# One number in a planner's price list: what a float32r matmul is said to cost

## The chip, the cores and the metric

The kernel runs on one core of a Trainium2 chip. The metric is the device time of one execution in microseconds (us), as the median of several runs; smaller is better. The engines are PE (TensorE: matmul), with its weight load PEld, DVE (VectorE), ACT (ScalarE), POOL (GpSimd) and SP (SyncE), which here issues the DMAs.

## The reference, cut to what matters

Two transformer blocks of two layers each, one after the other, on 256 tokens of width 1024, all in float32:

```
for i in range(2):                       # first block
    x = x + 0.5*g1 * swiglu(mod(rms(x)), wg, wu, wd)      # F = 2816
    x = x + g2 * (diff_attention(h) if i == 0 else spatial_gating(h))
    x = x + 0.5*g3 * swiglu(mod(rms(x)), wg, wu, wd)
    x = rms_norm(x, ln_out[i])
for i in range(2):                       # second block
    x = x + g1 * (hgrn2_mixer(h) if i == 0 else nsa_mixer(h))
    x = x + g2 * conv_ffn(mod(rms(x)), w_up, conv, w_down)
return rmsnorm(x, final_norm)
```

The shifts, scales and gates (`mod`, `g1` ...) come from `silu(c) @ ada_w`, whose weights are read once like all others.

## The kernel before, in words

The work falls into ten stages: feed-forward (0), differential attention (1), feed-forward (2, 3), spatial gating (4), feed-forward (5), hgrn2 (6), convolutional feed-forward (7), nsa (8), convolutional feed-forward (9). Every projection is computed with float32r operands (a float32 split into a rounded high part and a rest): hi·hi, hi·lo and lo·hi, three products where one would do. ACT copies a loaded weight tile `raw` to `whi`, DVE subtracts to get `wlo`; there are 4 buffers for `raw` and 6 each for `whi` and `wlo`. Activations are split in the same way: `h` to `hhi`, `hlo`, and `a32` or `oT` to `ahi`, `alo`.

Two widths of product occur. Up-projections that keep features on the partitions (`pg`, `pv`, `pa`, `pq`, `pf`, `px`, `pqk`) move 256 columns. Down-projections (`pd`) move 512 columns, as do the kernel's first `pgv`; the products that follow later norms half by half (`pgv`, `pig`, `px`) move 256. Between two stages stands a chain that no PE work of the next stage can pass: the last `pd`, residual on DVE (`gy`, `x`), sum of squares on ACT (`xs`), a power on POOL (`ss`), scaling (`xs`), transposes on PE (`xT`), modulation on ACT (`h`), the split on DVE (`hhi`, `hlo`), then the first product. The 256 tokens are taken in two halves, called first and second half here: `pd` products of the second half are kept back (by the table `SKEW`) so that they lie beside the chain of the first.

None of this is issued in the order in which it is written. Class `Plan` records every operation (`add`), gives it a price in ns (`price`, L289 to L320), and `order` (L322) plays the five engines forward: each engine takes the ready operation that was written first, is busy for its price, and its followers become ready after its end plus a delay from the table `LATE` (L196). Slots for buffers and PSUM tiles, the ACT tables, a DMA rate and a clock model for PE that doubles a price are played too. `emit` (L507) then issues each engine's instructions in the order that came out, which is why every row of the trace has L514 as its line. The hardware runs each engine's queue in that fixed order, with semaphores for what depends on other engines. So a price changes no instruction, only which one stands before which.

The line that is changed is the price of a PE product whose moving operand is float32r (L300 and L301). The other prices of PE stay: a transpose 109 ns, and a float32 product by its rows and columns.

Of the kernel before, what the change touches and what calls it, by code (L numbers as in the profile page):

```python
# [208 lines left out]
class Plan:  # L209
# [79 lines left out]
    def price(self, eng, method, args, kw, reads, writes):  # L289

        n = max(int(np.prod(v.shape[1:])) for v in (writes[-1:] if eng == "tensor" else reads + writes) or reads)
        if eng == "sync":
            v = (writes + reads)[0]
            size = int(np.prod(v.shape)) * 4
            return 450.0, size / 360.0
        if eng == "tensor":
            if method == "transpose":
                return 109.0, 60.0
            n = int(np.prod(args[2].shape[1:]))
            if args[2].tl.dtype == F32R:  # L300
                return n / 2.4 + 2.2, 60.0  # L301
            m = writes[0].shape[0]
            t = 4 * max(n, m) / 2.4
            return (t + 4.5 if m > 64 else t / 2 + 28.0 if m > 32 else t / 4 + 20.0), 60.0
        ps = any(v.tl.psum for v in reads + writes)
        if eng == "scalar":
            aps = sum(isinstance(kw.get(x), Vw) for x in ("scale", "bias", "accum_out"))
            return (51.0 if ps else 94.0) + n * 0.833 + 93.0 * aps, 40.0
        if eng == "gpsimd":
            if kw.get("op") == OP.pow:  # L310
                return 290.0 + 165.0 * n, 60.0
            return 200.0 + 0.7 * n, 60.0
        aps = 0
        if method in ("tensor_scalar", "scalar_tensor_tensor"):
            aps = sum(isinstance(v, Vw) for v in args[2:4 if method == "tensor_scalar" else 3])
        if method in ("tensor_copy", "tensor_scalar", "memset") and not ps:
            return 67.0 + 0.52 * n + 60.0 * aps, 20.0
        if method == "reciprocal":
            return 65.0 + 6.2 * n, 20.0
        return 70.0 + 1.04 * n + 60.0 * aps, 20.0  # L320
# [1626 lines left out]
```

## Time and profile before

| | before |
|---|---|
| median of 3 runs | 1718.03 us (1716.29 to 1719.7) |
| profiled execution | 1716.82 us |
| its span, first to last instruction | 1715.1 us |
| PE busy | 1677.9 us, 98% |
| DVE, ACT, POOL busy | 1309.9, 946.5, 65.3 us |
| mean granted clock of PE | 0.993 |

The profiled execution took 1.7 us more than its span, and 1.2 us less than the median of the runs. A busy engine in this table is one with an instruction in flight; PE's instructions overlap one another, so that the step from one product to the next, not the length of one, is what it costs.

### The profile page before, as it was taken

Reading aid. Unit: us, or ns where it says so; the run is one execution under the profiler, and the core shown is the slowest. Engines: PE = TensorE matmul, PEld = TensorE weight load, DVE = VectorE, ACT = ScalarE, POOL = GpSimd, SP = SyncE. Lnnn points to the kernel's source line nnn. Section 1 sums busy time; section 2 is a strip of 40 time slices with the busy share of each in tenths; the row PEclk is TensorE's granted clock in tenths of the full one; section 3 lists DMA queues with packets and bytes.
Section 4 is the critical chain, followed back from the end, with each engine's and each line's share of the span. In section 5 each row is a group of like instructions: output and inputs, shape, how many; then the busy total and the mean of one; then the engine's idle time right before and its main releaser. Section 6 shows DMA issues by size and latency. Waiting matters only on the chain.

```text
span 1715.1 us, 30950 instructions
## 1 busy us (share of the span) xinstructions
PE 1677.9 (98%) x12662; PEld 1510.6 (88%) x12662; DVE 1309.9 (76%) x1951; ACT 946.5 (55%) x1581; POOL 65.3 (4%) x60
## 2 busy tenths in 40 slices
PE   8999999999999999999999999999999999999998
PEld 6899789889988999789999879989998886689986
DVE  5877688876777888677777787889898557888754
ACT  4544366564445544364544368876554566766542
POOL 0000012100001000000000000000000000000000
PEclk9999999999999999999999999999999999999999
DMA  9988875667886998667689875347898566256662
GB/s 322 346 304 297 291 237 198 211 218 242 304 310 219 330 318 300 240 225 240 215 278 297 304 251 180 127 160 247 272 305 304 176 200 240 79 164 230 220 211 74
DMA packets 258191, 415.25 MB, mean 242 GB/s; under 512 B 12938, under 2 KB 204277, under 8 KB 257025
## 3 DMA queue, kind: packets, MB, share of 16 engines
q1 hardware_dynamic: 258049, 413.27, 71.4%
q8 instruction: 99, 1.62, 0.4%
q14 instruction: 43, 0.35, 0.1%
HBM read 412.14 MB, written 1.10 MB: 241 GB/s over the span
## 4 chain that ended last, share of the span: by engine, by line
PE 87%; DMA 4%; DVE 4%; ACT 3%; issue 1%; SPq 1%; POOL 1%; DVEq 0%; POOLq 0%; ACTq 0%
PE pd L514 22%; PE pv L514 21%; PE pg L514 12%; PE pa L514 7%; PE pgv L514 3%; PE pig L514 3%; PE pq L514 3%; PE pqk L514 2%; PE pf L514 1%; DVE wlo L514 1%; PE px L514 1%; ACT h L514 1%; DMA raw<-in_ffn_wu 1%; ACT whi L514 1%; PE no L514 1%
## 5 line engine op out<-in xcount | busy, mean ns | idle before, releaser
L514 ACT ACTIVATE whi<-raw 128x1024 fp32r<-128x1024 f32 x508 | 531.0, 1056 | 545.2 <-PE pd L514 144.2
L514 DVE TENSOR_TENSOR wlo<-raw,whi 128x1024 fp32r<-128x1024 f32 x508 | 612.0, 1220 | 221.4 <-ACT whi L514 219.1
L514 DVE SCALAR_TENSOR_TENSOR acc<-raw,csil,acc 128x1024 f32<-128x1024 f32 x192 | 245.9, 1281 | 18.1 <-DMA raw<-in_ada_w 15.6
L514 PE MATMUL pv<-hhi,wlo 128*128 128x256 f32 x896 | 252.5, 282 | 0.0
L514 PE MATMUL pv<-hhi,whi 128*128 128x256 f32 x896 | 252.2, 282 | 0.0
L514 PE MATMUL pv<-hlo,whi 128*128 128x256 f32 x896 | 252.1, 281 | 0.0
L514 PE MATMUL pd<-whi,ahi 128*128 128x512 f32 x604 | 238.9, 397 | 1.1 <-ACT ahi L514 0.5
L514 PE MATMUL pd<-wlo,ahi 128*128 128x512 f32 x604 | 238.0, 394 | 0.8 <-DVE wlo L514 0.8
L514 PE MATMUL pd<-whi,alo 128*128 128x512 f32 x604 | 237.3, 394 | 0.0
L514 PE MATMUL pg<-hhi,wlo 128*128 128x256 f32 x608 | 171.8, 283 | 0.7 <-DVE wlo L514 0.7
L514 PE MATMUL pg<-hhi,whi 128*128 128x256 f32 x608 | 172.1, 283 | 0.0
L514 PEld LDWEIGHTS pv<-hhi,whi 128*128 128x128 f32 x896 | 170.6, 190 | 0.8 <-issue 0.8
L514 PE MATMUL pg<-hlo,whi 128*128 128x256 f32 x608 | 171.4, 282 | 0.0
L514 PEld LDWEIGHTS pv<-hhi,wlo 128*128 128x128 f32 x896 | 170.6, 190 | 0.0
L514 PEld LDWEIGHTS pv<-hlo,whi 128*128 128x128 f32 x896 | 170.5, 190 | 0.0
L514 PEld LDWEIGHTS pd<-whi,ahi 128*128 128x128 f32 x604 | 113.4, 188 | 31.9 <-issue 4.5
L514 PEld LDWEIGHTS pd<-wlo,ahi 128*128 128x128 f32 x604 | 113.4, 188 | 26.6 <-DVE wlo L514 1.9
L514 PEld LDWEIGHTS pd<-whi,alo 128*128 128x128 f32 x604 | 113.5, 188 | 25.4
L514 PEld LDWEIGHTS pg<-hhi,whi 128*128 128x128 f32 x608 | 115.8, 190 | 3.0 <-issue 2.1
L514 PEld LDWEIGHTS pg<-hhi,wlo 128*128 128x128 f32 x608 | 115.8, 190 | 0.9 <-DVE wlo L514 0.9
L514 PEld LDWEIGHTS pg<-hlo,whi 128*128 128x128 f32 x608 | 115.7, 190 | 0.0
L514 PE MATMUL pa<-hhi,whi 128*128 128x256 f32 x352 | 99.3, 282 | 0.0
(361 smaller groups left out, 3136.8 us busy)
## 6 DMA issues: line engine op xcount, KB each, us to landing
raw<-in_ada_w SPq DMA_DIRECT2D x118, 1024.0 KB
raw<-in_ffn_wd SPq DMA_DIRECT2D x44, 1024.0 KB
raw<-in_ffn_w_up SPq DMA_DIRECT2D x44, 1024.0 KB
raw<-in_ffn_wg SPq DMA_DIRECT2D x41, 1024.0 KB
raw<-in_ffn_wu SPq DMA_DIRECT2D x41, 1024.0 KB
raw<-in_ffn_w_down SPq DMA_DIRECT2D x22, 1024.0 KB
raw<-in_hg_w_in SPq DMA_DIRECT2D x16, 1024.0 KB
raw<-in_attn_w_qkv SPq DMA_DIRECT2D x12, 1024.0 KB
```

The costliest lines, as they stand in the source:

```text
L514: f(*[real(v) for v in args], **{k: real(v) for k, v in kw.items()})
```

## The change

The price of a float32r product of n columns was n/2.4 + 2.2 ns, and is n/2.4 + 10 + n/78 ns: 108.9 becomes 119.9 ns at n = 256, and 215.5 becomes 229.9 ns at n = 512.

```diff
             if args[2].tl.dtype == F32R:
-                return n / 2.4 + 2.2, 60.0
+                return n / 2.4 + 10.0 + n / 78.0, 60.0
             m = writes[0].shape[0]
```

Each engine issues the same number of instructions of each kind before and after. What differs is their order, in many places on PE, ACT and DVE, in few on SP.

**At the end of attention (stage 1 to 2), PE.** `oT` transposes the last heads' output, `modt` and `modc` belong to the next stage's modulation, `pd` is attention's output projection. Before:

```order
L514 MATMUL pd<-wlo,ahi 128x512
L514 MATMUL o<-v,atT 128x128 x4
L514 MATMUL modt<-ident,sums 128x128 x4
L514 MATMUL pd<-whi,alo 128x512
L514 MATMUL pd<-whi,ahi 128x512
```

Then 13 more rows of `pd`, one product each, up to `oT`, and 25 after it before the transposes `xT` of the next stage. With the change:

```order
L514 MATMUL modc<-acc,ones 32x512 x4
L514 MATMUL pd<-whi,ahi 128x512
L514 MATMUL pd<-wlo,ahi 128x512
L514 MATMUL pd<-whi,alo 128x512
L514 MATMUL pd<-whi,ahi 128x512
L514 MATMUL pd<-wlo,ahi 128x512
L514 MATMUL oT<-ident,on 128x128 x4
L514 MATMUL modt<-ident,sums 128x128 x4
L514 MATMUL pd<-whi,alo 128x512
```

Between `o` and `oT` stand 12 `pd` and `modc` now, where 15 `pd` and `modt` stood, and 43 `pd` follow `oT` before `xT`, where 25 did.

**The same place on DVE**, where `x_96` is the first half of the tokens and `x_103` the second. Before:

```order
L514 TENSOR_TENSOR gy<-pd,gb 128x512
L514 TENSOR_TENSOR x_96<-x_96,gy 128x512
L514 TENSOR_TENSOR gy<-pd,gb 128x512
L514 TENSOR_TENSOR x_96<-x_96,gy 128x512
L514 TENSOR_TENSOR gy<-pd,gb 128x512
L514 TENSOR_TENSOR x_103<-x_103,gy 128x512
L514 TENSOR_SCALAR ss<-ss 128x1
L514 TENSOR_TENSOR gy<-pd,gb 128x512
L514 TENSOR_SCALAR xs<-x_96,ss 128x512
```

With the change:

```order
L514 TENSOR_TENSOR gy<-pd,gb 128x512
L514 TENSOR_TENSOR x_96<-x_96,gy 128x512
L514 TENSOR_TENSOR gy<-pd,gb 128x512
L514 TENSOR_TENSOR x_96<-x_96,gy 128x512
L514 TENSOR_SCALAR ss<-ss 128x1
L514 TENSOR_TENSOR gy<-pd,gb 128x512
L514 TENSOR_SCALAR xs<-x_96,ss 128x512
L514 TENSOR_TENSOR x_103<-x_103,gy 128x512
```

A `gy` and an `x` of the second half stand behind the `ss` of the first.

**At the start of hgrn2 (stage 5 to 6), DVE.** `xrow` is the row scaling of the norm at the end of the first block, `h_10700` and `h_10703` the modulated first half. Before:

```order
L514 TENSOR_TENSOR xrow<-x_103,raw 128x512
L514 TENSOR_TENSOR wlo<-raw,whi 128x1024
L514 TENSOR_TENSOR gy<-pd,gb 128x512
L514 CAST hhi<-h_10700 128x2x128
L514 TENSOR_TENSOR x_103<-x_103,gy 128x512
L514 CAST hhi<-h_10700 128x2x128
L514 TENSOR_TENSOR hlo<-h_10700,hhi 128x4x128
L514 CAST hhi<-h_10710 128x2x128 x2
L514 TENSOR_TENSOR hlo<-h_10710,hhi 128x4x128
L514 TENSOR_TENSOR xrow<-x_103,raw 128x512
L514 TENSOR_SCALAR ss_10681<-ss_10681 128x1
L514 TENSOR_TENSOR wlo<-raw,whi 128x1024
```

With the change:

```order
L514 TENSOR_TENSOR xrow<-x_103,raw 128x512
L514 TENSOR_TENSOR gy<-pd,gb 128x512
L514 TENSOR_TENSOR x_103<-x_103,gy 128x512
L514 TENSOR_TENSOR xrow<-x_103,raw 128x512
L514 CAST hhi<-h_10703 128x2x128 x2
L514 TENSOR_TENSOR hlo<-h_10703,hhi 128x4x128
L514 CAST hhi<-h_10714 128x2x128 x2
L514 TENSOR_TENSOR hlo<-h_10714,hhi 128x4x128
L514 TENSOR_TENSOR wlo<-raw,whi 128x1024 x2
```

(The change has five more rows, `ss`, `x_103` and `xs`, ahead of that last one.) The second half's `x` and `xrow` stand ahead of the first half's split now, and both `wlo` behind it. On PE, 25 `pig`, 8 `xT` and 71 `pig` stand where 47 `pig`, 4 `xT`, 1 `pig`, 4 `xT` and 48 `pig` stood (a single `pf` product among the last).

**In nsa (stage 8), PE.** `ph` is the hidden layer of the compression, `npT` transposes of scores, `pq` a query projection, `pkc` the first product that reads `ht`, the Silu of `ph`. Before:

```order
L514 MATMUL ph<-raw,cw_15273 64x75
L514 MATMUL npT<-ident,lg 128x128 x5
L514 MATMUL pq<-hhi,whi 128x256
L514 MATMUL pq<-hlo,whi 128x256
L514 MATMUL pq<-hhi,wlo 128x256
L514 MATMUL pkc<-ht,cw_14615 64x60
L514 MATMUL pvc<-cw_14615,ht 32x64 x4
```

With the change:

```order
L514 MATMUL pq<-hlo,whi 128x256
L514 MATMUL pq<-hhi,wlo 128x256
L514 MATMUL pq<-hhi,whi 128x256
L514 MATMUL pq<-hlo,whi 128x256
L514 MATMUL pq<-hhi,wlo 128x256
L514 MATMUL pkc<-ht,cw_14617 64x60
L514 MATMUL pvc<-cw_14617,ht 32x64 x4
```

These are the last 5 of 16 `pq` that stand between `npT` and `pkc` now; 13 of them moved there from ahead of `ph`.

## Rows read from the trace of the kernel before

**Rows 1.** The page, busy time, share of the span and instructions of each engine.

```profile
span 1715.1 us, 30950 instructions
PE 1677.9 (98%) x12662; PEld 1510.6 (88%) x12662; DVE 1309.9 (76%) x1951; ACT 946.5 (55%) x1581; POOL 65.3 (4%) x60
```

**Rows 2.** The chain in order of time: start us, us, what; stage 2.

```profile
417.24 5.55 PE pv L514 x48
422.79 5.76 PE pg L514 x48
...
489.01 36.71 PE pd L514 x159
```

**Rows 3.** Waits of PE, whole span: us in total, times, longest.

```profile
PE xT L514 <- DVE xs L514: 4.7, 4, 2.6
...
PE pkc L514 <- ACT ht L514: 1.6, 1, 1.6
...
PE pv L514 <- DVE hhi L514: 0.4, 1, 0.4
```

**Rows 4.** Windows: us, busy us of PE, PEld, DVE, ACT, POOL; PE's clock; DMA.

```profile
348.16:354.99 6.83, 5.73 (x27) 5.73 (x28) 5.04 (x12) 5.61 (x17) 0.56 (x1) 0.50 0.04 6
1440.43:1447.25 6.82, 6.82 (x28) 3.43 (x27) 5.02 (x21) 5.29 (x14) 0.00 (x0) 0.50 0.89 328
```

**Rows 5.** The chain in order of time, stage 1 to 2.

```profile
341.33 0.70 DVE gy L514
...
344.71 0.69 DVE x L514
...
346.25 1.95 ACT xs L514 x5
```

**Rows 6.** Waits of PE from 318 to 356 us.

```profile
PE pd L514 <- ACT ahi L514: 0.5, 1, 0.5
```

**Rows 7.** The chain in attention, first pair of heads.

```profile
249.08 3.56 PE pqk L514 x29
...
256.46 0.11 PE pT L514
```

**Rows 8.** Timeline of DVE, same place: start us, us, engine line op.

```profile
249.10 1.22 DVE L514 TENSOR_TENSOR wlo<-raw,whi 128x1024 fp32r<-128x1024 f32 x1
...
254.60 0.60 DVE L514 SCALAR_TENSOR_TENSOR at<-lg,smx,at 128x128 f32<-128x128 f32 x2
```

**Rows 9.** The chain in order of time, stage 4 to 5.

```profile
824.77 0.73 ACT xs L514
...
825.55 1.09 PE xT L514 x8
```

**Rows 10.** Waits of the DMA queue SP from 880 to 990 us.

```profile
SPq L514 <- ACT grow L514: 2.8, 1, 2.8
```

**Rows 11.** Timeline, stage 5 to 6, [idle before and its releaser].

```profile
1018.63 0.29 DVE L514 CAST hhi<-h 128x256 fp32r<-128x256 f32 x1 [0.23 <-ACT h L514]
...
1022.39 1.22 DVE L514 TENSOR_TENSOR wlo<-raw,whi 128x1024 fp32r<-128x1024 f32 x1
...
1023.66 0.38 PE L514 MATMUL pig<-wlo,hhi 128*128 128x256 f32 x1 [0.50 <-DVE wlo L514]
```

**Rows 12.** The chain in hgrn2, first pair of heads.

```profile
1057.54 1.72 PE pig L514 x13
1059.26 1.34 PE o L514 x12
```

**Rows 13.** Timeline of DVE, same place.

```profile
1057.96 0.92 DVE L514 COPY st<-sc 32x128 f32<-32x128 f32 x4
```

**Rows 14.** Waits of PE from 1150 to 1172 us, stage 6 to 7.

```profile
PE xT L514 <- DVE xs L514: 1.3, 1, 1.3
```

**Rows 15.** The chain in order of time, nsa.

```profile
1436.70 1.28 ACT L514
...
1437.99 0.32 ACT ht L514
```

## The prediction

> **What bounds the kernel now.** First the busy shares: PE has something in flight in 1677.9 of 1715.1 us, and no other engine comes near [rows 1]. So 37 us are all that PE is idle, and most of the rest is products that the change doesn't touch. The waits of PE, taken together next, are small and many: 23 lines, from 4.7 us for `xT` waiting on `xs` down to 0.4 us, which add up to 29 us [rows 3]. The reader is to see that no single wait is worth 0.3% of the time. Third, the clock: in a few stretches the granted clock is 0.50, the 1.2 GHz level; two of them are 6.8 us long, one after the long wait at the end of attention, one in nsa after the wait of `pkc` [rows 4]. With PE busy for 5.73 and 6.82 us in them, half of that, 2.9 and 3.4 us, is what the lower level cost. So what an order can move at all is some 29 us of waits and a handful of us of clock; it can also make new waits, with no such bound, wherever a product that covered a chain is taken away.
>
> **Is the new price right?** 48 products of 256 columns take 5.55 to 5.76 us, which is 116 to 120 ns each, and 159 of 512 columns 36.71 us, or 231 ns [rows 2]. The new price says 119.9 and 229.9, the old said 108.9 and 215.5: the planner believed PE to be 7 to 10% faster than it is. The change does what it says. A rule speaks against it: the Trainium skill, "TensorE: Matmul & The Clock Gate", section "Back-to-back issue gap", gives N/2.4 + 2.5 ns for an isolated product, almost the old price, and for streams of weight load and product about 131 ns at N = 512, far below both. By that page's figure the 159 products would take an estimated 21 us and the change would go the wrong way; this trace has 36.71 us for them, so here the measurement decides, and the price is now right.
>
> A right price for PE doesn't make a right plan. The other prices and delays are as they were, and PE's queue runs in the planned order. With products too cheap, the planner put about 10% more of them between a product that starts a chain on ACT, DVE and POOL and the one that waits for its end, and on the chip that was spare time wherever a chain is longer than planned. The new price takes that spare time away; it also moves work at places where the old plan had a hole. So the sum goes by places. I compared the order on PE, DVE, ACT and SP at each border between stages and inside attention, hgrn2 and nsa. Feed-forward interiors are alike apart from which product follows which, and are put at nothing: there 48 products follow 48 with no wait in the chain.
>
> **The places** (minus is time lost; in brackets both ends).
>
> Start and stage 0 to 1. Three reads of modulation stand one or so 512-column product earlier, 3 x 0.23 = 0.7 us if each waits; `xT` of the second half comes after 34 instead of 37 products, 3 x 0.12 = 0.4. Together -1.1 [0 to -2.2, twice that].
>
> Attention, first pair of heads. From the end of `pl` (249.08) to the end of the `at` that `pT` transposes (255.20) passed 6.1 us, and 57 `pqk` covered them, so that `pT` at 256.46 had 1.3 us to spare [rows 7, 8]. Now 24 `pqk` and two `plam` cover it, 24 x 0.12 + 0.2 = 3.1 us. The chain gets shorter too: the `wlo` of 1.22 us in its middle [rows 8] stands elsewhere, and ACT's table load ahead of it, for which I take another 0.5. That leaves 4.4, and -1.3. Two later pairs have 10 and 5 products fewer: -0.4. Together -1.7 [0 to -3.1, where the chain shortens so little that all 33 products but the 1.3 us are missed].
>
> End of attention. 43 `pd` follow `oT` where 25 did. Before, from the first `gy` (341.33) to the end of its `xs` the chain ran to some 346.6, and DVE did a `gy` and an `x` of the second half (0.6 + 0.69 us) ahead of `ss` in it [rows 5]; `xT` waited 2.6 us of the 4.7 in [rows 3] there. Now those 1.3 us stand behind, which leaves 4.0 us of chain, and some 24 `pd`, 24 x 0.23 = 5.5 us, cover it: +2.6. The wait of `pd` for `ahi`, 0.5 us [rows 6], has `modt` in it: +0.5. The clock fell there after that wait; I count half of its 2.9 us, +1.5. Against that a `wlo` stands between the first two `hhi`, -1.2. Together +3.4 [0 to +6.0, all of wait and clock].
>
> Stage 4 to 5. `xT` of the second half started right when `xs` was there (825.50 against 825.55) [rows 9], so no cover was spare. It comes after 27 instead of 35 products now: 8 x 0.12, -1.0 [0 to -1.0].
>
> Stage 5. SP stood 2.8 us at a store that waited for `grow` [rows 10], with weight loads queued behind it; that store is issued after loads now. Transfers set the end there only in part, so half: +1.4 [0 to +2.8].
>
> Stage 5 to 6. The first `hhi` came at 1018.63; now `x` and `xrow` of the second half, 0.68 us each, stand ahead of it [rows 11], and DVE gets there about 1.1 us later; PE waits for it already, so all of this shows. The `wlo` of 1022.39, on which `pig` waited 0.5 us [rows 11], moves behind the second half's `ss` and `xs`: about 1.3 us later. What comes back is 0.4, since 23 `pig` of the first half are still there to cover the second half's split. Together -2.0 [0 to -4.9, with a half-clock stretch like the first of rows 4, 2.9 us, brought on by the holes].
>
> Heads of hgrn2. In the first pair `st` was complete at 1058.88 and `o` started at 1059.26 [rows 12, 13]: under 0.4 us to spare behind 78 products. 67 are left for the first three pairs, 11 x 0.12 = 1.3 us less. With up to 1.0 to spare elsewhere I take 0.8 for each: -2.4 [0 to -3.9].
>
> Stage 6 to 7. `xT` waits 1.3 us for `xs` [rows 14]; `ss` comes one `gy`, `x` pair earlier: half, +0.7 [0 to +2.0 with some clock].
>
> nsa. `pkc` waits for `ht`, which comes behind ACT's step of 1.28 us at 1436.70 [rows 15]: 1.6 us [rows 3]. 13 more `pq`, 13 x 0.12 = 1.6 us, lie there now: +1.6. Of the 3.4 us of clock after it I count 0.4, since the small products that follow are the same. Together +2.0 [-1.0, since `ph` comes 1.6 us earlier and may wait for its input; to +5.0 with all the clock].
>
> **The sum**: -1.1 - 1.7 + 3.4 - 1.0 + 1.4 - 2.0 - 2.4 + 0.7 + 2.0 = -0.7 us. Against the profiled execution's own 1716.82 (span 1715.1 and 1.7 around it) this is 1717.5. That execution was 1.2 below the median of the runs; on the median, 1718.0 + 0.7 = **1718.7 us**. The lower ends add up to -16, the upper to +16; as the places fail independently, their half-widths (1.1, 1.5, 3, 0.5, 1.4, 2.5, 2, 1, 3) combine to some 6 us, which 8 times in 10 is about 8, and the scatter of a median, 1.7, and the places not read come on top.
>
> **The rivals.** 0.2%, 3.4 us, is about what a measurement of this kernel can tell from no change.
>
> *No change that can be told*, my forecast: PE's products are the same, gains and losses are of one size. Its own range is 1714.6 to 1721.5. Chance 0.38.
>
> *Faster: the two half-clock stretches go with the holes ahead of them.* For it: both follow a wait that the new order covers, by 5.5 us against 4.0, and by 1.6 against 1.6. Against it: in the first, PE is busy for only 5.73 of 6.83 us [rows 4], so later waits lie in it that stay; in nsa the small products stay. It takes the full 2.9 + 3.4 instead of 1.9, so +4.4: sum +3.7, 1714.3; with SP's other half and the head chains holding, 1711. It decides as soon as `xT` at the end of attention starts without a wait. Chance 0.30.
>
> *Slower: the start of hgrn2 opens a hole.* DVE's order puts two whole steps of the second half ahead of the first half's split. If `hhi` comes 1.1 us and both `wlo` over 1.2 us late, PE stands twice within 8 us, and the clock falls as it did after the holes of [rows 4]: -4.9 instead of -2.0, and with the heads at -3.9 the sum is -5.1, or 1723. It decides from about 1 us of wait at the first `pig`. If attention loses its 3.1 too, 1725. Chance 0.32.
>
> *The page's rule*, products faster than either price: [rows 2] exclude it; no chance of its own.
>
> The range, 8 in 10, is **1709 to 1729**: 9 us below and 10 above the forecast. Faster by over 0.2% 0.30, within 0.2% 0.38, slower by over 0.2% 0.32.
>
> **What would show it.** Products at 120 and 231 ns as before, the same counts. The wait of `xT` at the end of attention gone, and the one of `pkc`; new waits, 1 to 1.5 us each, at the first `pT`, at `xT` of stage 5, at the first `pig` and behind its `wlo`, under 1 us at `o` in hgrn2. PE's idle time between 35 and 40 us. I am wrong if the chip's clock falls in stretches where it was full, if a chain that I held to be longer than planned is not, or if a place that I put at nothing, such as a DMA stretch of stage 5 or the interior of a feed-forward, moves by several us.

## The result, and the profile after

The changed kernel took 1736.16 us (median of 5 runs, 1735.35 to 1740.5) against 1716.78 us of the kernel before (5 runs, 1712.31 to 1719.7): a ratio of 1.0127, 95% interval 1.0111 to 1.0143 (the two medians alone give 1.0113). It is slower by 1.3%, outside the range of 1709 to 1729.

First the busy shares on the page of the changed kernel, to be read against [rows 1]:

```profile
span 1734.2 us, 31004 instructions
PE 1678.8 (97%) x12662; PEld 1511.9 (87%) x12662; DVE 1310.0 (76%) x1951; ACT 946.5 (55%) x1581; POOL 61.9 (4%) x60
```

Every engine but POOL (61.9 against 65.3 us) is busy for the same time to within 1.3 us. The span is 19.1 us longer, and PE is idle for 55.4 us in place of 37.2: 18.2 us of the loss is PE standing.

Next the waits of PE over the span (us in total, times, longest), which answer to [rows 3]:

```profile
PE modt L514 <- ACT sums L514: 12.0, 3, 5.9
PE xT L514 <- DVE xs L514: 5.3, 6, 1.9
PE pgv L514 <- DVE hhi L514: 4.6, 4, 1.8
PE cols L514 <- DMA rows<-in_ffn_conv_w: 3.6, 1, 3.6
...
PE pst L514 <- DVE X L514: 1.9, 4, 0.5
PE pTc L514 <- DVE lc L514: 1.6, 1, 1.6
PE qkT L514 <- DVE qn L514: 1.6, 3, 0.8
PE pig L514 <- DVE hhi L514: 1.6, 1, 1.6
```

and of the kernel before, three rows that did not stand among [rows 3]:

```profile
PE pgv L514 <- DVE hhi L514: 3.3, 4, 1.3
...
PE pig L514 <- DVE hhi L514: 1.0, 2, 0.6
...
PE modt L514 <- ACT sums L514: 0.8, 1, 0.8
```

`xT` and the `hhi` that `pgv` waits for behind the norms, which the prediction worked on, moved by 0.6 and 1.3 us. What is new is `modt` waiting for `sums` (12.0 against 0.8) and `cols` for a DMA (3.6). `modt` belongs to the modulation of the next stage, which is streamed beside the feed-forward: loads `raw<-in_ada_w`, `acc` on DVE, `modc` on PE, `sums` on ACT, `modt` on PE.

The longest of these waits is in the down-projection of stage 5. The timeline of ACT there in the changed kernel (start us, us, engine, operation, and in brackets the idle time before it and what ended it), then PE's rows:

```profile
987.99 2.01 ACT L514 ACTIVATE whi<-raw 128x1024 fp32r<-128x1024 f32 x2 [6.40 <-DMA raw<-in_ffn_wd]
993.07 2.01 ACT L514 ACTIVATE whi<-raw 128x1024 fp32r<-128x1024 f32 x2 [3.07 <-DMA raw<-in_ffn_wd]
996.94 2.01 ACT L514 ACTIVATE whi<-raw 128x1024 fp32r<-128x1024 f32 x2 [1.87 <-DMA raw<-in_ffn_wd]
1003.28 2.19 ACT L514 ACTIVATE dhi<-raw 128x512 fp32r<-128x512 f32 x4 [4.33 <-DMA raw<-in_ffn_wd]
1008.29 2.01 ACT L514 ACTIVATE whi<-raw 128x1024 fp32r<-128x1024 f32 x2 [2.81 <-DMA raw<-in_ffn_wd]
1011.64 2.00 ACT L514 ACTIVATE whi<-raw 128x1024 fp32r<-128x1024 f32 x2 [1.35 <-DMA raw<-in_ffn_wd]
1014.51 2.00 ACT L514 ACTIVATE whi<-raw 128x1024 fp32r<-128x1024 f32 x2 [0.86 <-DMA raw<-in_hg_w_in]
1016.42 0.58 ACT L514 ACTIVATE sums<-modc 128x512 f32<-128x512 f32 x1
...
1010.71 0.40 PE L514 MATMUL pd<-dlo,ahi 128*128 128x512 f32 x1
1017.05 1.11 PE L514 MATMUL modt<-ident,sums 128*128 128x128 f32 x4 [5.94 <-ACT sums L514]
```

The last product of `modc` starts at 1009.2 us and takes 0.6, so `sums` could have run at 1010. But six copies of weights stand ahead of it on ACT, behind `dhi`. Each of these three pairs waited for a DMA: the first was running at 1010, the loads of the other two had not landed. So `sums`, 0.58 us of work, runs at 1016.42, and PE's queue stands behind `modt` meanwhile. The same place in the kernel before:

```profile
994.84 2.20 ACT L514 ACTIVATE dhi<-raw 128x512 fp32r<-128x512 f32 x4 [3.90 <-DMA raw<-in_ffn_wd]
997.58 2.01 ACT L514 ACTIVATE whi<-raw 128x1024 fp32r<-128x1024 f32 x2 [0.54 <-DMA raw<-in_ffn_wd]
1000.27 0.60 ACT L514 ACTIVATE sums<-modc 128x512 f32<-128x512 f32 x1 [0.69 <-PE modc L514]
1000.77 2.00 ACT L514 ACTIVATE whi<-raw 128x1024 fp32r<-128x1024 f32 x2
1003.73 2.01 ACT L514 ACTIVATE whi<-raw 128x1024 fp32r<-128x1024 f32 x2 [0.97 <-DMA raw<-in_hg_w_in]
```

Of the six copies behind `dhi`, two stand ahead of `sums` there and four behind it, and `sums` waited for PE, not for a load. The loads are no slower in the changed kernel. The DMA queue's packets and MB, and the time they took as a share of the span, before (of 1715.1 us) and after (of 1734.2 us):

```profile
q1 hardware_dynamic: 258049, 413.27, 71.4%
```

```profile
q1 hardware_dynamic: 258049, 413.27, 70.9%
```

What differs is what the plan believed. In the planner's own times for the changed kernel (worked out by its `order` alone, without the chip), the last of the six loads is there at 978.66 us and `modc` is ready to be copied at 981.76, 3.1 us later. On the chip that load came 4.7 us after `modc` was done. So the plan gave the copies the earlier places, because it held the loads to be there sooner relative to PE's products. The two other waits of `modt`, 3.1 and 2.9 us, are of the same kind. The one at 904 stands behind a pair of copies on ACT:

```profile
904.41 2.00 ACT L514 ACTIVATE whi<-raw 128x1024 fp32r<-128x1024 f32 x2 [4.01 <-DMA raw<-in_ffn_wg]
906.32 0.58 ACT L514 ACTIVATE sums<-modc 128x512 f32<-128x512 f32 x1
```

The one at 621.8 comes through DVE:

```profile
622.10 1.28 DVE L514 SCALAR_TENSOR_TENSOR acc<-raw,csil,acc 128x1024 f32<-128x1024 f32 x1 [3.48 <-DMA raw<-in_ada_w]
623.30 0.68 DVE L514 TENSOR_TENSOR a<-pv,sg 128x512 f32<-128x512 f32 x1
...
624.02 0.63 ACT L514 ACTIVATE ahi<-a 128x512 fp32r<-128x512 f32 x1 [3.48 <-DVE a L514]
624.56 0.58 ACT L514 ACTIVATE sums<-modc 128x512 f32<-128x512 f32 x1
```

An `acc` waits 3.5 us for its load, `a` stands behind it on DVE, `ahi` behind `a` on ACT, `sums` behind `ahi`. How general it is shows in the waits of DVE, of before and of after:

```profile
DVE acc L514 <- DMA raw<-in_ada_w: 19.1, 23, 1.9
```

```profile
DVE acc L514 <- DMA raw<-in_ada_w: 67.5, 55, 4.1
```

Two of the three waits of `modt` also bring a stretch at the lower clock. Windows of the changed kernel (columns as in [rows 4]), the first three from the wait at 1010 on, the fourth after that at 621.8, the fifth after that at 904, where the clock stayed full:

```profile
1010.00:1017.00 7.00, 1.10 (x5) 0.56 (x3) 5.50 (x6) 4.78 (x6) 0.00 (x0) 0.85 1.01 319
1017.00:1021.00 4.00, 3.95 (x12) 3.27 (x13) 1.30 (x3) 0.00 (x0) 0.00 (x0) 0.50 1.02 326
1021.00:1028.00 7.00, 7.00 (x30) 5.68 (x29) 3.00 (x5) 1.45 (x4) 0.00 (x0) 0.95 0.35 114
...
625.20:632.00 6.80, 6.80 (x45) 6.80 (x46) 4.42 (x6) 1.70 (x2) 0.00 (x0) 0.75 0.84 275
...
907.00:914.00 7.00, 7.00 (x60) 7.00 (x61) 4.93 (x8) 3.24 (x4) 0.00 (x0) 1.00 1.04 372
```

A clock of 0.75 over 6.8 us is 3.4 us at the 1.2 GHz level, an estimated 1.7 us lost with PE busy throughout. With the wait of 3.1 us that makes the 4.9 which the table below has for the place, to 0.1. Around 1017 it is 2.1 + 4.0 + 0.7 = 6.8 us, of which the first 2.1 lie in the wait. Over the whole span there is little more of it than before: the mean granted clock is 0.992 against 0.993.

### The profile page after: what moved, and what is told of

It reads as the page before. It is cut to its first block, busy times and chain, and to the rows that moved or that the text cites. A ratio compares the mean times of both kernels' runs of the same rounds, so it can differ in the third digit from the quotient of the medians.

```text
span 1734.2 us, 31004 instructions
## 1 busy us (share of the span) xinstructions
PE 1678.8 (97%) x12662; PEld 1511.9 (87%) x12662; DVE 1310.0 (76%) x1951; ACT 946.5 (55%) x1581; POOL 61.9 (4%) x60
```

## The experiments

Two theories and a rival. **A**: the old prices of products and of loads were short by about the same share, so that the planner had them in the right proportion; with products alone put right, loads come early in the plan, and ACT and DVE take what hangs on loads ahead of what PE waits for. **B**: the same for the prices of ACT, DVE and POOL. **C**: any other order has a few long waits somewhere, by chance. The kernels below change only prices or delays of the planner, so all do the same work. Each ran beside the kernel before on the same chip (medians 1713.5 to 1714.5 us), so ratios are compared.

**Loads priced up with the products.**

```diff
-            return 450.0, size / 360.0
+            return 450.0, size / 330.0
```

> The changed kernel with the planner's rate for transfers at 330 instead of 360 bytes per ns, so that loads are priced up by the 9% by which products were. Theory A (the old prices of products and of loads were short by about the same share and cancelled; with products alone made longer, the plan lets ACT and DVE take loads ahead of work that PE waits for, and the loads come late): the three waits of modt for sums (12.0 us) and those of cols for rows (4.8 us) mostly go, and the time is 1718 to 1724 us. Theory B (it is the prices of ACT, DVE and POOL that had been cancelled): those waits stay, 1733 to 1738. Theory C (each order has a few long waits at places that fall by chance): any value from 1715 to 1740, with long waits elsewhere.

1718.24 us, ratio 1.0026 (1.0015 to 1.0036). The waits of `modt` are down to 1.3 us and those of `cols` to 0.5, and `acc` waits 24.3 us for loads in place of 67.5. That is what A said and not B: with loads priced up beside products, four fifths of the loss go.

**Engines priced up, loads not.** Prices and delays of ACT, DVE and POOL times 1.09.

```diff
+        cost, late = self.price_of(eng, *rest)
+        return (cost * SLOW, late * SLOW) if eng in ("scalar", "vector", "gpsimd") else (cost, late)
...
+SLOW = 1.09
+LATE = {e: {k: v * SLOW for k, v in d.items()} if e != "sync" else d for e, d in LATE.items()}
...
-                    cost += 1300.0
+                    cost += 1300.0 * SLOW
```

> The changed kernel with the planner's prices of ACT, DVE and POOL, their table load and their delays times 1.09, loads as they were. Theory A: the waits of modt and cols stay, the small ones at heads and norms go, 1728 to 1733 us. Theory B: all go, 1715 to 1722. Theory C: any value from 1715 to 1740.

1732.11 us, ratio 1.0107 (1.0089 to 1.0124): the time that A gave, but not for A's reasons. Its waits:

```profile
PE xT L522 <- DVE xs L522: 9.0, 6, 3.5
PE modt L522 <- ACT sums L522: 5.2, 2, 3.0
```

`modt` waits 5.2 us in place of 12.0, `cols` 1.0 in place of 3.6 for `in_ffn_conv_w`, and the places of loads lose 3.9 us in place of 17.6 (table below), where A had them stay. But the waits at the norms, which A had go, grew, and the other places together lost 10.5 us more than in the changed kernel. B had all the loss go. The loads are late here too:

```profile
DVE acc L522 <- DMA raw<-in_ada_w: 53.7, 47, 3.3
```

So late loads alone don't cost PE its time, and dearer engines in the plan take most of that cost away as well. Why they do is not shown.

**The other way round: the old price, loads cheaper.** The kernel before with `size / 395.0`.

> The kernel before with the planner's rate for transfers at 395 instead of 360 bytes per ns: products and engines priced as before, loads 9% cheaper. Theory A: waits of modt for sums and of cols for rows as in the changed kernel appear, 1725 to 1735 us. Theory B: as before, 1714 to 1720. Theory C: any value from 1712 to 1740.

1723.03 us, ratio 1.0051 (1.0034 to 1.0069). Slower, and in part by the waits that A names, though by less than it gave:

```profile
PE modt L514 <- ACT sums L514: 3.9, 2, 2.3
```

With no product's price touched, making loads early in the plan gives the same fault, in a smaller size: 7.2 us at the places of loads.

**Both corrections**, loads at 330 and engines times 1.09.

> The changed kernel with both edits, loads at 330 and ACT, DVE, POOL times 1.09, so that all prices stand to each other about as in the kernel before. Theories A and B: the time of before, 1713 to 1721 us, with no wait over 3 us. Theory C: any value from 1712 to 1740, as the order still differs in many places.

1710.82 us, ratio 0.9985 (0.9975 to 0.9995): a little better than A and B gave, with one wait just over their 3 us (3.1, `xT`). With the right price among its companions the loss is gone; the 0.15% gained is no more than the empty change below gains.

**The wait itself.** What follows `sums` is held to be ready 6 us later in the plan, which moves `modt` and little else.

```diff
+                if e == "scalar" and any(tl.kw["name"] == "modc" for tl in op.tiles):
+                    end += 6000.0
                 op.fin = end
```

> The changed kernel with one edit in the planner: what follows the copy of modc to sums on ACT is held to be ready 6 us later, so that modt is placed later on PE; ACT's and DVE's orders and PE's else stay nearly as in the changed kernel (43 rows of PE differ). Theory A (sums stands on ACT behind copies of weights whose loads come late, and PE's queue stands behind modt): the 12.0 us of waits at modt go and nothing takes their place, 1723 to 1727 us. Rival (the late loads hold up PE anyway, and modt is only where it shows): the wait moves to the next product that needs a weight, 1733 to 1737.

1726.48 us, ratio 1.0080 (1.0055 to 1.0106). Of the waits of `modt` 0.7 us are left, and the one of `cols` stays, as that edit can't reach it:

```profile
PE pig L516 <- DVE hhi L516: 3.8, 1, 3.8
...
PE cols L516 <- DMA rows<-in_ffn_conv_w: 3.2, 1, 3.2
```

The profiled span is 1722.7 us, 11.5 below the changed kernel's, for 12.0 us of waits taken away; by the two ratios (1.0127 and 1.0080) it is some 8 us. PE was held up by the order, not by weights that it lacked, as the rival would have it; 2.2 us came back at the first `pig`, which waits 3.8 in place of 1.6, and the lower clock that followed the waits of `modt` went with them.

**A later landing in place of a lower rate.**

```diff
-                    dma_free = end = max(dma_free, t + 1100.0) + op.late
+                    dma_free = end = max(dma_free, t + 2000.0) + op.late
```

> The changed kernel with the planner's time from issue to the earliest landing of a load at 2000 instead of 1100 ns, and the rate left at 360. If the loads come late because each takes longer from issue to landing than planned (four buffers that wait for each other), this does as much as the lower rate: 1716 to 1723 us. If it is the rate alone: 1730 to 1737.

1714.70 us, ratio 1.0004 (0.9989 to 1.0019). A little under the 1716 to 1723 of its first case: either correction of the loads takes most or all of the loss away. Which of them is nearer to the chip is not settled by these: this one keeps 3.4 us of waits at `modt` and 2.2 at `cols` and gains elsewhere.

**One width at a time.** The new price for 512 columns alone, then for 256 alone.

```diff
-                return n / 2.4 + 10.0 + n / 78.0, 60.0
+                return n / 2.4 + (10.0 + n / 78.0 if n > 256 else 2.2), 60.0
```

> The new price for products of 512 columns alone, the old one for 256. Theory A: the wait of modt in the down-projection of stage 5 (5.9 us) stays, those in the up-projections go: 1719 to 1725 us. Theory C (chance): any value.

> The new price for products of 256 columns alone, the old one for 512. Theory A: the waits of modt and cols in up-projections (11 us) and the losses in the heads of hgrn2 and attention stay, that in the down-projection of stage 5 goes: 1726 to 1732 us. Theory C: any value.

1715.97 us, ratio 1.0016 (1.0001 to 1.0032), and 1736.30 us, 1.0133 (1.0111 to 1.0155): both outside A's ranges, below the first and above the second. The 256-column price carries the whole loss. I had the wait in stage 5's down-projection with the 512-column one; it shows with neither width alone, and the other waits were larger instead (`modt` 7.9 us, `cols` 4.7).

**Both corrections, the loads by the later landing** (the edits of the second and the sixth kernel).

> The changed kernel with ACT, DVE and POOL priced times 1.09 and the landing of loads at 2000 ns: both corrections, the second in the form that did most. Theory A with B: no wait of modt or cols over 2.5 us, none lost in the heads of hgrn2, 1705 to 1713 us, under the kernel before. Theory C (chance): any value from 1710 to 1740.

1723.18 us, ratio 1.0053 (1.0036 to 1.0070): a miss by 10 us. No `modt` or `cols` over 2.5 us is left and the heads lose little, as expected, but `xT` waits for `xs` at two borders:

```profile
PE xT L522 <- DVE xs L522: 9.3, 5, 3.6
```

So part of C is true: at the borders of stages an order gains or loses some 4 us each for reasons that neither A nor B foresees.

**An empty change**, 0.6 ns more on each product of the kernel before (`n / 2.4 + 2.8`).

> The kernel before with 0.6 ns more on each float32r product (109.5 and 216.1 ns), which reorders many places and corrects nothing. Theories A and B: a twentieth of the change, 1713 to 1718 us on a chip where before takes 1713.5. Theory C: up to 10 us away from it on either side.

1709.49 us, ratio 0.9983 (0.9966 to 1.0000): below what A and B gave, and within C's. So much does an order move by chance: 2.9 us by the ratio and 5.0 by the medians here, mostly at two places (below).

**Half of the change.**

> The changed kernel with half of the addition: 114.4 and 222.7 ns. Theory A: loads come late by half as much in the plan's time and the chains lose half of their cover, 1720 to 1729 us. Theory C: any value, as likely outside these as between them.

1723.66 us, ratio 1.0050 (1.0033 to 1.0067), between the two as A gave, with 6.8 us of waits at `modt`.

**By places.** For each kernel's profile: the time at which PE's n-th instruction starts, less that of the kernel before, and of this the growth from one end of a place to the other, in us (worked out from PE's records; plus is lost). Columns are the changed kernel and the experiments in the order above, from 1 to 11; "loads" names the places where a modulation or its columns are finished beside a feed-forward. Each column is one execution, and its sum can be some us from what the ratio gives (column 7: -7.4 against +2.7).

```
place          after    1    2    3    4    5    6    7    8    9   10   11
start            1.4  1.7  1.4  2.8  2.5  0.7  0.4  0.5  0.3  1.9  0.0  0.6
loads, 147 us    5.4 -0.0  1.3  1.0 -0.1  3.4  3.8 -0.0  7.3  1.8  0.0  1.0
attention        1.1  3.0  2.8  3.3 -0.4  2.7 -0.8 -0.8  2.4 -1.8 -0.9  2.5
stage 1 to 2    -5.6 -5.6 -0.4 -4.1 -5.2 -6.0 -5.9 -4.6 -5.5 -1.5 -6.0 -5.7
loads, 608 us    4.9 -0.1  0.0  0.0 -0.0 -0.0 -0.2  0.0  5.1  0.0  0.0  0.0
stage 4 to 5     1.9  0.2 -0.2 -0.0 -0.1  1.6 -0.3  1.9  0.1 -0.5 -0.0 -0.0
loads, 878 us    1.3 -0.8  0.5  3.8 -1.2 -2.0  0.7 -2.0  4.7 -1.8 -0.3 -0.1
loads, 963 us    6.0 -2.1  2.1  2.4  0.5  1.9 -2.3 -2.3 -1.7 -2.3 -2.3  6.3
hgrn2, start     1.6  3.2  0.8  0.5  0.7  3.8  1.7  1.6  0.8  1.4  0.9  0.8
hgrn2, heads     2.8  2.7  1.2 -0.0  0.6  2.8  2.8 -0.4  2.8  0.9  0.0  0.1
stage 6 to 7     0.2 -0.1  3.8  0.1  1.6  0.2 -0.1 -0.4  2.4  2.8  1.4  2.9
nsa             -4.1 -1.2  0.4 -2.0 -1.6 -4.0 -4.6 -1.8 -2.3  3.0 -0.5 -4.6
all             19.1  4.6 16.8 11.7 -4.3  7.6 -2.8 -7.4 17.7  6.0 -8.1  6.0
```

The four rows of loads hold 17.6 of the 19.1 us; 2.2 lie between the places listed. In sum the four are at 0 or less wherever loads are priced up (1, 4, 9, and 2.0 in 6) or the 256-column price is the old one (7, 10), and positive where loads are cheap against products (3.9 in 2, 7.2 in 3, 15.4 in 8, 7.2 in 11). The waits of `acc` for its loads part the orders in the same way: 13.6 to 24.3 us in the kernel before, 1, 4, 7, 9 and 10, 35.3 in 6, and 51.9 to 83.2 in the changed kernel, 2, 3, 5, 8 and 11. So how late the loads are goes with their price against that of the 256-column products. What PE pays for it, 3.3 us (5) to 17.6, hangs on what the order puts behind them, and there C is right in part.

## Why the prediction was wrong

**The step that failed** is "Feed-forward interiors are alike apart from which product follows which, and are put at nothing". The reason given was that there 48 products follow 48 with no wait in the chain. On PE `modt` did move by 1 to 4 products only, but it is the end of a chain too, over `sums` on ACT, and 0.8 us of wait stood there before already. What stands ahead of `sums` on ACT, and when that can run on the chip, was not asked: in place of nothing the four places lost 17.6 us. The prediction had half of the mechanism, that a right price beside the other, old prices doesn't make a right plan. It worked this out for the prices of engines and not for those of loads; its list of what would prove it wrong named the place.

The places that it did work out came near in their numbers, as the first column shows against the terms of the sum, less so in their mechanisms.

- Start and stage 0 to 1: -1.1 forecast, 1.4 us lost at the start; the rest lies in the row of attention. Attention: -1.7, lost 1.1, but not by the chain forecast: `pT` has no wait, and `qkT`, which was not named, waits 1.6 us for `qn`.
- End of attention: +3.4, gained 5.6, near the upper end. The wait of `xT` there is down to 0.3 us and the clock stayed full, as this window of the changed kernel shows:

```profile
351.00:358.00 7.00, 5.68 (x44) 5.04 (x42) 6.43 (x13) 6.50 (x14) 1.41 (x1) 1.00 0.01 2
```

  But the empty change gains 6.0 there too. The gain is a matter of which row DVE takes first, and no merit of the right price.
- Stage 4 to 5: -1.0, lost 1.9, more than its own end of -1.0 and by another wait: `xT` of the second half has none, `pgv` waits 1.8 us for `hhi`, and the clock fell for 3.4 us, as this window shows:

```profile
830.60:834.00 3.40, 3.40 (x17) 3.40 (x17) 2.98 (x6) 2.96 (x8) 1.06 (x1) 0.50 0.02 5
```

- Stage 5, the store that held up SP: +1.4, nothing to be seen. The wait for `grow` [rows 10] is no longer in SP's list for that stretch, and loads were late all the same.
- Start of hgrn2: -2.0, lost 1.6: the wait of `pig` for `hhi` is 1.6 us in place of 1.0, and the second half's `xT` waits 0.9 us.
- Heads: -2.4, lost 2.8. The mechanism is right, the row is another: `pst` waits for `X` (1.9 us), not `o` for `st`. The loss follows the 256-column price (2.8 with it alone, -0.4 without it) and shrinks to 0.6 to 1.2 where the engines are priced up: here B holds.
- Stage 6 to 7: +0.7, lost 0.2.
- nsa: +2.0, gained 4.1; `pkc` no longer waits, `pTc` does, 1.6 us, and the clock stayed full.

Without that store, whose place is among the loads, they were forecast at 2.1 lost together; measured, they come to 0.7 gained. That these sums lie near each other is in part luck: three of the waits forecast did not come (`pT`, `xT` of stage 5, `o`), others stand in their place, and the largest gain comes with an empty change too. The chance of 0.32 for slower was held for a rival, the start of hgrn2. Its wait at the first `pig` did come, but the clock stayed full, and the place lost 1.6 us and not the 4.9 of the rival.

Open stays what the loads' prices are short of: rate or time to landing. The windows don't settle it: at a DMA share over 1 the one at 1017 has 326 GB/s, below the planner's 360 bytes per ns, and the one at 907 has 372, above it; and the later landing did as much as the lower rate. Open stays too why dearer engines cut the loss at the loads.

## What to carry to other kernels

A planner's prices work by their proportion. Before one of them is put right, ask which others were wrong in the same direction, transfers first, and change them together: alone, the right price cost 1.3%; with loads priced up too, the loss was 0.3% (by the rate) or could not be told from none (by the landing). With engines priced up as well it was 0.15% gained in the one form and 0.5% lost in the other, so the companions take this loss away but don't promise a gain. And when an order changes, read for each product that waits what stands ahead of its producer on that producer's queue, and whether that can run yet: a 0.58 us copy stood behind four others whose loads had not landed, and PE stood for 5.9 us.

## What the runs showed that was not expected

An order that differs by chance moved this kernel by 0.17% (interval 0 to 0.34%): a price 0.6 ns higher, which corrects nothing, gave -6.0 us at one border of stages. Differences of a few us between two plans are told from chance only place by place.

PE idle for 2.2 us of 12 at the start of hgrn2 kept the full clock, and so did the unbroken wait of 2.9 us at 904, while the unbroken waits of 3.1 and 5.9 us brought 3.4 and 6.8 us at 0.50, as the windows of the result show. The start of hgrn2 in the changed kernel:

```profile
1030.00:1042.00 12.00, 9.80 (x57) 8.09 (x55) 9.28 (x22) 9.33 (x22) 1.94 (x4) 1.00 0.27 78
```
